# A trunk kernel with split float32 matmuls: two views of each activation tile at different SBUF offsets, and two tiles placed on other addresses

## The chip, the cores and the metric

The kernel runs on one core of a Trainium2 chip. The metric is the device time of one execution in microseconds; three runs of the kernel before were timed, and their median is the time before.

## What is computed

A decoder trunk of two layers on one sequence of 256 tokens with a model width of 2048, all in float32. Layer 0 mixes with a gated DeltaNet, layer 1 with differential attention on keys and values that are projected from the stream after layer 0. Each layer has an MLP of width 8192 with a squared ReLU, and a per-layer embedding that is projected and gated. Cut to what matters:

```python
for i in range(DEPTH):                       # DEPTH = 2
    xn = rmsnorm(h, norm_mix[i])
    if i < N_A:                              # layer 0: 16 query/key heads, 32 value heads of 128
        h = h + gated_deltanet(xn, gdn_w_in[i], gdn_conv_w[i], gdn_a_log[i], gdn_dt_bias[i], gdn_norm_w[i], gdn_w_out[i])
    else:                                    # layer 1: 8 heads, all read the shared keys and values
        h = h + diff_attention(xn, k_shared, v_shared, diff_w_q[j], ..., diff_subln_w[j], diff_w_o[j], i)
    hn = rmsnorm(h, norm_mlp[i])
    h = h + jnp.square(jax.nn.relu(hn @ mlp_w1[i])) @ mlp_w2[i]
    gate = jax.nn.sigmoid(rmsnorm(h, norm_ple[i]) @ ple_w_gate[i])
    h = h + (p[i] @ ple_w_proj[i]) * gate
    if i == N_A - 1:
        kv = rmsnorm(h, kv_norm) @ w_kv      # shared keys (2048 columns) and values (2048 columns)
return rmsnorm(h, final_norm)
```

## The kernel before

**Split products.** Every large product runs as three matmuls on values that are split in a high and a low part: high by high, high by low, low by high. `chunk` (line 116) loads 1 MB of a weight matrix into a tile `raw` by a DMA on SP's queue, and for each 1024 columns of it ScalarE writes the high part `whi` (line 130) and VectorE the low part `wlo` (line 131). `raw`, `whi` and `wlo` have three buffers each. The activations lie transposed in pairs of tiles of 128 partitions by 16 x 256 values: `xha` and `xla` (the pair `xa`, allocated in `run`), `xhb` and `xlb` (the pair `xb`, in `attention`), `hidh` and `hidl` (the hidden layer of the MLP), `oh` and `ol` (four rows of 256 values, the normalised output of two DeltaNet heads).

**Two forms of product.** In `g2` (line 136) the weights are the stationary operand, 128 columns at a time, and the activations move, 256 columns per matmul:

```python
nc.tensor.matmul(o, hi[:, k, cs], xh[:, kt], ...)   # line 149
nc.tensor.matmul(o, hi[:, k, cs], xl[:, kt], ...)   # line 150
nc.tensor.matmul(o, lo[:, k, cs], xh[:, kt], ...)   # line 151
```

In `g1` (line 154) the activations are stationary, 128 tokens at a time, and the weights move, 512 columns per matmul (lines 165 to 167). Every matmul has a weight load of its own, which loads its stationary operand.

**What runs in which form.** `g2` with `xa`: in layer 0 the gates (48 matmuls), the keys (768), the queries and values of eight groups of heads (768 and 1536); the first half of both MLPs (6144); the shared keys (768). That is 10032 matmuls. `g2` with `xb`: the query projection of layer 1 (768). `g1` with `xa`: the projection z of the eight groups (768), the gate of the embedding step `ple` in both layers (768), the shared values (384). `g1` with `xb`: the output projection of the attention, whose input `oT` is written into the pair `xb` once the queries are done (384). `g1` with `oh` and `ol`: the output projection of the DeltaNet (768). `g1` with `hidh` and `hidl`: the second half of the MLPs (6144).

**Order.** In `deltanet` a written plan sets the order of the steps: keys and inverses of triangular blocks first, then for each of eight groups the unit step `unit` (two heads in turn: a chain of small 128-column matmuls on TensorE with a subtraction on VectorE after each, lines 409 to 444), the next group's queries and values, z, and the output projection of the group before. The tile framework's scheduler orders the instructions of each engine, and it places matmuls of the next group's projections between the steps of a unit's chain. After it come MLP, `ple`, `attention`, MLP, `ple` and `final`.

**Sums of squares.** `rstd` (line 170) takes eight Square activations on ScalarE, whose elementwise output goes to a tile `junk` with two buffers, then a reduction on VectorE, a square root on ScalarE and a reciprocal on VectorE.

Of the kernel before, what the change touches and what calls it, by code (L numbers as in the profile page):

```python
# [10 lines left out]
F32 = mybir.dt.float32  # L11
# [5 lines left out]
P = 128  # L17
# [13 lines left out]
EPS = 1e-6  # L31
NEG = -1e30
LAM_INIT = 0.8 - 0.6 * math.exp(-0.3 * 1)
POST = 1.0 - LAM_INIT


class Trunk:
# [78 lines left out]
    def chunk(self, src, kn, cols):  # L116
        """src [kn*128, cols] -> list of kn*cols/1024 (hi, lo, first k tile, k tiles)"""
        nc = self.nc
        raw = self.wraw.tile([P, 2048], F32, name="raw")
        size = kn * cols  # L120
        nc.sync.dma_start(out=raw[:, :size].rearrange("p (k n) -> p k n", k=kn),
                          in_=src.rearrange("(k p) n -> p k n", p=P))
        res = []
        step = 1024 // cols
        for k0 in range(0, kn, step):
            kk = min(step, kn - k0)
            sl = raw[:, k0 * cols:(k0 + kk) * cols]
            hi = self.whl.tile([P, 1024], F32R, name="whi")[:, :kk * cols]
            lo = self.whl.tile([P, 1024], F32R, name="wlo")[:, :kk * cols]
            nc.scalar.copy(hi, sl)  # L130
            nc.vector.tensor_tensor(lo, sl, hi.bitcast(F32), ALU.subtract)  # L131
            res.append((hi.rearrange("p (k n) -> p k n", k=kk),
                        lo.rearrange("p (k n) -> p k n", k=kk), k0, kk))
        return res

    def g2(self, x, w, nk, c0, cols, kn):
        """channel-major product: returns banks, bank i holds column tiles 2i, 2i+1 as [128, 2, 256]"""
        nc = self.nc
        xh, xl = x
        nct = cols // P  # L140
        banks = [self.bank() for _ in range((nct + 1) // 2)]
        for kb in range(0, nk, kn):
            for hi, lo, k0, kk in self.chunk(w[kb * P:(kb + kn) * P, c0:c0 + cols], kn, cols):
                for k in range(kk):
                    kt = kb + k0 + k
                    for ct in range(nct):
                        o = banks[ct // 2][:, (ct % 2) * T:(ct % 2) * T + T]
                        cs = slice(ct * P, ct * P + P)
                        nc.tensor.matmul(o, hi[:, k, cs], xh[:, kt], start=kt == 0 and ct % 2 == 0, stop=False, skip_group_check=True)  # L149
                        nc.tensor.matmul(o, hi[:, k, cs], xl[:, kt], start=False, stop=False, skip_group_check=True)  # L150
                        nc.tensor.matmul(o, lo[:, k, cs], xh[:, kt], start=False, stop=kt == nk - 1, skip_group_check=True)  # L151
        return banks

    def g1(self, x, w, nk, c0, kn=4, pool=None):
        """token-major product with 512 columns from c0: returns one bank per token tile"""
        nc = self.nc
# [13 lines left out]
    def rstd(self, h, scale=1.0 / D, epscol=0):  # L170
        """reciprocal root mean square per token: [128, 2]"""
        nc = self.nc
        ss = self.small.tile([P, NT, 4], F32, name="ss")
        for b in range(4):
            for t in range(NT):
                junk = self.small.tile([P, 512], mybir.dt.bfloat16, name="junk")
                nc.scalar.activation(junk, h[t][b], AF.Square, accum_out=ss[:, t, b:b + 1])
        r = self.small.tile([P, NT], F32, name="rs", bufs=4)
        nc.vector.tensor_reduce(r, ss, axis=AX.X, op=ALU.add)
        nc.scalar.activation(r, r, AF.Sqrt, scale=scale, bias=self.eps[:, epscol:epscol + 1])  # L180
        nc.vector.reciprocal(r, r)
        return r

    def transposed(self, h, outs):
        """outs: list of (x tile, weight columns); writes hi/lo of h transposed, scaled per channel"""
        nc = self.nc
# [12 lines left out]
    def xpair(self, pool, which):  # L199
        return (pool.tile([P, KD, T], F32R, name="xh" + which), pool.tile([P, KD, T], F32R, name="xl" + which))  # L200

    def rowcast(self, r, dst):
        """[128, 2] per-token values -> dst [128, 256] along the free dimension on every partition"""
        nc = self.nc
# [7 lines left out]
    def gates(self, x, pool, tmp):  # L212
        """beta and cumulative log decay: token-major [128, 2, 64] and rows in DRAM"""
        nc, d = self.nc, self.d
# [38 lines left out]
    def conv(self, banks, dst, ch0):  # L253
        """banks of channel-major projections -> dst(i) [128, 256]: causal conv of four taps"""
        nc = self.nc
# [16 lines left out]
    def key_norms(self, half, kT, pool):  # L272
        """diagonal 32x32 blocks of the key products of eight heads; norms and row scales from their diagonals"""
        nc = self.nc
# [12 lines left out]
        nc.vector.tensor_tensor(dg, Gc, self.i32[:, None, :].to_broadcast([P, 16, 32]), ALU.mult)  # L287
        ss = pool.tile([P, 8, 2], F32, name="kss", bufs=1)
        nc.vector.tensor_reduce(ss.rearrange("p h c -> p (h c)"), dg, axis=AX.X, op=ALU.add)
# [7 lines left out]
    def invert(self, half, Gc, one, pool):  # L297
        """inverses of the 32x32 diagonal blocks of eight key heads, all value heads and both halves of the sequence"""
        nc = self.nc
# [73 lines left out]
    def unit(self, u, kT, q, qn, vt, pool):  # L373
        """one query/key head with its two value heads: normalised token-major output [128, (half, head), 128]"""
        nc = self.nc
# [217 lines left out]
    def ple(self, h, layer, w, pool):  # L593
# [11 lines left out]
        nc.vector.tensor_tensor(pl, ps, ph.bitcast(F32), ALU.subtract)  # L605
        self.transposed(h, [(self.xa, w)])
        r = self.rstd(h)
        for nb in range(4):
            gate = self.g1(self.xa, d["ple_w_gate"][layer], KD, nb * 512)
            pr = self.g1((ph, pl), d["ple_w_proj"][layer], 2, nb * 512, kn=2, pool=self.mis)  # L610
# [9 lines left out]
    def attention(self, h):  # L620
        nc, tc, d = self.nc, self.tc, self.d
        with ExitStack() as c:
            pool = c.enter_context(tc.tile_pool(name="att", bufs=2))
            one = c.enter_context(tc.tile_pool(name="att1", bufs=1))
            xb = self.xpair(one, "b")
            self.transposed(h, [(xb, self.w_mix1), (self.xa, self.w_kv)])
# [27 lines left out]
            v = [one.tile([P, D], F32, name=f"v{t}") for t in range(NT)]  # L654
            oT = xb

# [27 lines left out]
            def values(hd, aT):  # L684
# [4 lines left out]
                nc.tensor.matmul(po[:, T:], aT[:, 2 * P:], v[1][:, vs], start=False, stop=True, skip_group_check=True)  # L689
                ss = pool.tile([P, 2], F32, name="oss")  # L690
                o = pool.tile([P, 512], F32, name="o")
# [50 lines left out]
    def run(self, stop=None):  # L742
# [6 lines left out]
        self.constants()  # L749
        self.xa = self.xpair(self.main, "a")  # L750
        steps = [("mix0", lambda: self.deltanet(h))]
# [39 lines left out]
```

## Time and profile before

| | us |
|---|---|
| three runs | 2990.04, 2992.25, 2991.72 |
| median | 2991.72 |
| span of the profiled execution, first to last instruction | 2988.6 |

The profile gives the span of its execution and no separate time for it; the median of the runs is 3.1 us above the span, and that is what lies around it.

| engine | busy us | share of the span |
|---|---|---|
| TensorE, matmuls | 2951.5 | 99% |
| TensorE, weight loads | 2667.5 | 89% |
| VectorE | 1783.0 | 60% |
| ScalarE | 1449.6 | 49% |
| GpSimd | 57.9 | 2% |

How to read it: matmuls are pipelined, so one matmul's recorded time (some 280 ns for 256 columns) is longer than the distance to the next one's start, and a busy share of 99% does not tell how fast TensorE goes. Its pace, the distance from one matmul's start to the next one's, is read from a stretch that holds one kind of matmul alone: its length divided by the number of starts in it. The stages follow each other in time: the DeltaNet to about 930 us, MLP of layer 0 from 938 to 1652, `ple` to 1752, queries of layer 1 from 1774 to 1853, shared keys from 1853 to 1945, values and attention to 2083, its output projection to 2151, MLP of layer 1 from 2158 to 2872, `ple` and the end.

### The profile page before, as it was taken

Reading aid. Unit: us, or ns where it says so; the run is one execution under the profiler, and the core shown is the slowest. Engines: PE = TensorE matmul, PEld = TensorE weight load, DVE = VectorE, ACT = ScalarE, POOL = GpSimd, SP = SyncE. Lnnn points to the kernel's source line nnn. Section 1 sums busy time; section 2 is a strip of 40 time slices with the busy share of each in tenths; the row PEclk is TensorE's granted clock in tenths of the full one; section 3 lists DMA queues with packets and bytes.
Section 4 is the critical chain, followed back from the end, with each engine's and each line's share of the span. In section 5 each row is a group of like instructions: output and inputs, shape, how many; then the busy total and the mean of one; then the engine's idle time right before and its main releaser. Section 6 shows DMA issues by size and latency. Waiting matters only on the chain.

```text
span 2988.6 us, 44778 instructions
## 1 busy us (share of the span) xinstructions
PE 2951.5 (99%) x18730; PEld 2667.5 (89%) x18730; DVE 1783.0 (60%) x2324; ACT 1449.6 (49%) x1947; POOL 57.9 (2%) x64
## 2 busy tenths in 40 slices
PE   8999999999999999999999999999999999999998
PEld 8999889988988998989988889987899899898886
DVE  7879766666666555555555564467555555555555
ACT  5655555545545443444434553367444444344454
POOL 0011000000000000000000000000000000000000
PEclk9999999999999999999999999999999999999999
DMA  6654544445445555555565556544555565555654
GB/s 195 203 170 140 171 159 148 145 162 163 141 142 175 183 182 196 184 189 192 183 196 190 171 179 194 183 160 142 186 184 183 187 194 184 193 183 188 211 169 155
DMA packets 289595, 527.19 MB, mean 176 GB/s; under 512 B 25966, under 2 KB 44560, under 8 KB 289264
## 3 DMA queue, kind: packets, MB, share of 16 engines
q1 hardware_dynamic: 288160, 521.77, 54.2%
q8 instruction: 147, 2.41, 0.3%
q0 software_dynamic: 816, 2.03, 0.2%
q10 hardware_dynamic: 416, 0.53, 0.1%
q14 instruction: 56, 0.46, 0.0%
HBM read 520.03 MB, written 4.26 MB: 175 GB/s over the span
## 4 chain that ended last, share of the span: by engine, by line
PE 95%; DVE 3%; ACT 1%; DMA 1%; issue 0%; POOL 0%; ACTq 0%; SPq 0%; DVEq 0%
PE accb L165 16%; PE accb L166 16%; PE accb L167 16%; PE accb L150 14%; PE accb L151 14%; PE accb L149 14%; PE misb L426 2%; DVE wlo L131 1%; PE misb L409 1%; PE misb L431 1%; ACT whi L130 0%; PE misb L441 0%; PE misb L192 0%; PE misb L418 0%; PE misb L359 0%; ACT xha L196 0%
## 5 line engine op out<-in xcount | busy, mean ns | idle before, releaser
L131 DVE TENSOR_TENSOR wlo<-raw,whi 128x1024 fp32r<-128x1024 f32 x970 | 1189.9, 1228 | 1019.5 <-ACT whi L130 1018.4
L130 ACT CAST whi<-raw 128x1024 fp32r<-128x1024 f32 x970 | 1018.0, 1050 | 1337.3 <-PE accb L167 673.2
L149 PE MATMUL accb<-xha,whi 128*128 128x256 f32 x3344 | 953.9, 286 | 0.8 <-ACT whi L130 0.8
L150 PE MATMUL accb<-xla,whi 128*128 128x256 f32 x3344 | 952.6, 285 | 2.0 <-DVE xla L197 2.0
L151 PE MATMUL accb<-xha,wlo 128*128 128x256 f32 x3344 | 951.8, 285 | 0.2 <-DVE wlo L131 0.2
L150 PEld LDWEIGHTS accb<-xla,whi 128*128 128x128 f32 x3344 | 641.1, 192 | 2.8 <-DVE xla L197 2.6
L149 PEld LDWEIGHTS accb<-xha,whi 128*128 128x128 f32 x3344 | 640.9, 192 | 1.5 <-ACT whi L130 1.0
L151 PEld LDWEIGHTS accb<-xha,wlo 128*128 128x128 f32 x3344 | 640.7, 192 | 0.4 <-DVE wlo L131 0.4
L165 PE MATMUL accb<-whi,hidh 128*128 128x512 f32 x1024 | 398.7, 389 | 0.0
L166 PE MATMUL accb<-wlo,hidh 128*128 128x512 f32 x1024 | 398.6, 389 | 0.0
L167 PE MATMUL accb<-whi,hidl 128*128 128x512 f32 x1024 | 398.6, 389 | 0.0
L165 PE MATMUL accb<-whi,xha 128*128 128x512 f32 x640 | 253.5, 397 | 0.9 <-ACT xha L196 0.9
L166 PE MATMUL accb<-wlo,xha 128*128 128x512 f32 x640 | 252.5, 394 | 0.1
L167 PE MATMUL accb<-whi,xla 128*128 128x512 f32 x640 | 251.6, 394 | 0.0
L167 PEld LDWEIGHTS accb<-whi,hidl 128*128 128x128 f32 x1024 | 192.3, 188 | 39.9
L165 PEld LDWEIGHTS accb<-whi,hidh 128*128 128x128 f32 x1024 | 192.3, 188 | 39.8
L166 PEld LDWEIGHTS accb<-wlo,hidh 128*128 128x128 f32 x1024 | 192.3, 188 | 39.5
L165 PEld LDWEIGHTS accb<-whi,xha 128*128 128x128 f32 x640 | 120.3, 188 | 25.7 <-ACT xha L196 2.2
L166 PEld LDWEIGHTS accb<-wlo,xha 128*128 128x128 f32 x640 | 120.6, 188 | 24.9 <-DVE wlo L131 1.4
L167 PEld LDWEIGHTS accb<-whi,xla 128*128 128x128 f32 x640 | 120.2, 188 | 23.6
L165 PE MATMUL accb<-whi,oh 128*128 128x512 f32 x256 | 101.3, 396 | 0.8 <-ACT oh L466 0.8
L166 PE MATMUL accb<-wlo,oh 128*128 128x512 f32 x256 | 101.4, 396 | 0.0
(276 smaller groups left out, 2614.5 us busy)
## 6 DMA issues: line engine op xcount, KB each, us to landing
raw<-mlp_w SPq DMA_DIRECT2D x256, 1024.0 KB, 5.2
raw<-gdn_w_in SPq DMA_DIRECT2D x97, 1024.0 KB, 5.1
raw<-gdn_w_out SPq DMA_DIRECT2D x32, 1024.0 KB, 5.0
raw<-ple_w_gate SPq DMA_DIRECT2D x32, 1024.0 KB, 5.0
raw<-w_kv SPq DMA_DIRECT2D x32, 1024.0 KB, 5.3
raw<-diff_w_q SPq DMA_DIRECT2D x16, 1024.0 KB, 5.1
raw<-diff_w_o SPq DMA_DIRECT2D x16, 1024.0 KB, 5.0
gcb<-gcd SPq DMA_DIRECT2D x16, 256.0 KB, 4.3
```

The costliest lines, as they stand in the source:

```text
L130: nc.scalar.copy(hi, sl)
L131: nc.vector.tensor_tensor(lo, sl, hi.bitcast(F32), ALU.subtract)
L149: nc.tensor.matmul(o, hi[:, k, cs], xh[:, kt], start=kt == 0 and ct % 2 == 0, stop=False, skip_group_check=True)
L150: nc.tensor.matmul(o, hi[:, k, cs], xl[:, kt], start=False, stop=False, skip_group_check=True)
L151: nc.tensor.matmul(o, lo[:, k, cs], xh[:, kt], start=False, stop=kt == nk - 1, skip_group_check=True)
L165: nc.tensor.matmul(banks[t], xh[:, kt, ts], hi[:, k], start=kt == 0, stop=False)
L166: nc.tensor.matmul(banks[t], xh[:, kt, ts], lo[:, k], start=False, stop=False)
L167: nc.tensor.matmul(banks[t], xl[:, kt, ts], hi[:, k], start=False, stop=kt == nk - 1)
L409: nc.tensor.matmul(ps[:, n * P:(n + 1) * P], DB[:, n], av[:, n // 2, 2 * (n % 2)], start=True, stop=True)
L426: nc.tensor.matmul(ps[:, h * P:(h + 1) * P], NTt[:, 2 * h + c], X[:, h * P:(h + 1) * P], start=True, stop=True)
L431: nc.tensor.matmul(ps[:, h * P:(h + 1) * P], UB[:, 2 * h + c], X[:, h * P:(h + 1) * P], start=True, stop=True)
```

## The change

The pairs `xa` and `xb` get tiles that are 512 bytes longer per partition (128 values more), and `xpair` gives two views of each pair: one that starts 112 values (448 bytes) into the tile, and one that starts at its first byte. The first view takes the name `self.xa` (and `xb`) and serves everything but `ple` and the attention's output; the second view, `self.xs`, is what `ple` writes and reads, and the second view of `xb` is `oT`. So `g2` always reads the activations at the shifted start, z and the shared values read them there too, as stationary operand, and the gate of `ple` and the attention's output projection read from the unshifted start.

```diff
+SHIFT = 112
...
     def xpair(self, pool, which):
-        return (pool.tile([P, KD, T], F32R, name="xh" + which), pool.tile([P, KD, T], F32R, name="xl" + which))
+
+        tiles = [pool.tile([P, KD * T + 128], F32R, name=n + which) for n in ("xh", "xl")]
+        return tuple(tuple(t[:, o:o + KD * T].rearrange("p (k t) -> p k t", k=KD) for t in tiles) for o in (SHIFT, 0))
...
-        self.xa = self.xpair(self.main, "a")
+        self.xa, self.xs = self.xpair(self.main, "a")
...
-        self.transposed(h, [(self.xa, w)])
+        self.transposed(h, [(self.xs, w)])
...
-            gate = self.g1(self.xa, d["ple_w_gate"][layer], KD, nb * 512)
+            gate = self.g1(self.xs, d["ple_w_gate"][layer], KD, nb * 512)
...
-            xb = self.xpair(one, "b")
+            xb, oT = self.xpair(one, "b")
...
-            oT = xb
...
-                junk = self.small.tile([P, 512], mybir.dt.bfloat16, name="junk")
+                junk = self.small.tile([P, 512], mybir.dt.bfloat16, name="junk", bufs=1)
...
-        ss = pool.tile([P, 8, 2], F32, name="kss", bufs=1)
+        ss = pool.tile([P, 32], F32, name="kss", bufs=1)[:, :16].rearrange("p (h c) -> p h c", c=2)
...
-                ss = pool.tile([P, 2], F32, name="oss")
+                ss = pool.tile([P, 16], F32, name="oss")[:, :2]
```

The last three edits change sizes: `junk` gives up one of its two buffers of 1024 bytes, which pays for the longer pair `xa`, and `kss` and the attention's `oss` grow, which moves the tiles behind them. The built programs place the tiles so (byte offset in a partition, and its rest by 1024, by 512 and by 128; the weights' buffers `raw`, `whi`, `wlo` lie on multiples of 4096 in both):

```
                           before                       changed
xha as g2, z, V read it    86016    0   0   0           86464  448 448  64
xla as g2, z, V read it   102400    0   0   0          103360  960 448  64
xha as ple reads it        86016    0   0   0           86016    0   0   0
xla as ple reads it       102400    0   0   0          102912  512   0   0
xhb as g2 reads it        140736  448 448  64          141248  960 448  64
xlb as g2 reads it        157120  448 448  64          158144  448 448  64
oT, high part             140736  448 448  64          140800  512   0   0
oT, low part              157120  448 448  64          157696    0   0   0
oh                        220480  320 320  64          220544  384 384   0
ol                        224576  320 320  64          224640  384 384   0
hidh (both buffers)       122112  256 256   0          122112  256 256   0
```

In the DeltaNet most of the small tiles move by 64 bytes: `vt`, `X`, `Y`, `E`, `NTt`, `DB` and `UB` from multiples of 128 to 64 past one, `vc`, `qsq`, `o` and the keys the other way.

TensorE's instructions stand in the same order in both programs. With one buffer of `junk` the scheduler places a few instructions of VectorE and ScalarE otherwise where `ple` begins. VectorE there, before (`rs<-ss` is the reduction of `rstd`, `rs<-rs` its reciprocal, `xla<-misb,cols,xha` the low part of the transposed stream):

```order
L605 TENSOR_TENSOR pl<-misb,ph 128x512
L197 SCALAR_TENSOR_TENSOR xla<-misb,cols,xha 128x256 x13
L179 TENSOR_REDUCE rs<-ss 128x2
L131 TENSOR_TENSOR wlo<-raw,whi 128x1024
L197 SCALAR_TENSOR_TENSOR xla<-misb,cols,xha 128x256 x2
L181 RECIPROCAL rs<-rs 128x2
```

and in the changed program:

```order
L608 TENSOR_TENSOR pl<-misb,ph 128x512
L198 SCALAR_TENSOR_TENSOR xla<-misb,cols,xha 128x256 x3
L180 TENSOR_REDUCE rs<-ss 128x2
L198 SCALAR_TENSOR_TENSOR xla<-misb,cols,xha 128x256 x10
L182 RECIPROCAL rs<-rs 128x2
L132 TENSOR_TENSOR wlo<-raw,whi 128x1024
```

The reduction moves ahead of ten of the low parts, and the reciprocal ahead of one split of weights and two low parts. ScalarE at the same place, before (`junk,ss<-h` is the Square, `rs<-rs,eps` the square root):

```order
L177 ACTIVATE junk,ss<-h_81 128x512
L177 ACTIVATE junk,ss<-h_85 128x512
L196 ACTIVATE xha<-misb,cols 128x256 x10
L130 CAST whi<-raw 128x1024
L196 ACTIVATE xha<-misb,cols 128x256 x2
L180 ACTIVATE rs<-rs,eps 128x2
```

and in the changed program:

```order
L178 ACTIVATE junk,ss<-h_81 128x512
L178 ACTIVATE junk,ss<-h_85 128x512
L197 ACTIVATE xha<-misb,cols 128x256 x4
L181 ACTIVATE rs<-rs,eps 128x2
L197 ACTIVATE xha<-misb,cols 128x256 x6
L131 CAST whi<-raw 128x1024
```

The square root moves ahead of eight high parts and one cast of weights.

## Rows read from the trace of the kernel before

**Rows 1.** The page: TensorE's busy time, and its granted clock in 40 slices.

```profile
PE 2951.5 (99%) x18730; PEld 2667.5 (89%) x18730; DVE 1783.0 (60%) x2324; ACT 1449.6 (49%) x1947; POOL 57.9 (2%) x64
...
PEclk9999999999999999999999999999999999999999
```

**Rows 2.** The page: the chain that ended last, by engine, and by line.

```profile
PE 95%; DVE 3%; ACT 1%; DMA 1%; issue 0%; POOL 0%; ACTq 0%; SPq 0%; DVEq 0%
PE accb L165 16%; PE accb L166 16%; PE accb L167 16%; PE accb L150 14%; PE accb L151 14%; PE accb L149 14%; PE misb L426 2%; DVE wlo L131 1%; PE misb L409 1%; PE misb L431 1%; ACT whi L130 0%; PE misb L441 0%; PE misb L192 0%; PE misb L418 0%; PE misb L359 0%; ACT xha L196 0%
```

**Rows 3.** Groups of TensorE by line and shape: count, busy us, mean ns, idle before.

```profile
L149 PE MATMUL accb<-xha,whi 128*128 128x256 f32 x3344 | 953.9, 286 | 0.8 <-ACT whi L130 0.8
...
L165 PE MATMUL accb<-whi,xha 128*128 128x512 f32 x640 | 253.5, 397 | 0.9 <-ACT xha L196 0.9
...
L165 PE MATMUL accb<-whi,oh 128*128 128x512 f32 x256 | 101.3, 396 | 0.8 <-ACT oh L466 0.8
...
L149 PE MATMUL accb<-xhb,whi 128*128 128x256 f32 x256 | 70.7, 278 | 2.4 <-ACT xhb L196 2.4
...
L165 PE MATMUL accb<-whi,xhb 128*128 128x512 f32 x128 | 51.3, 401 | 0.0
```

**Rows 4.** Stretches of g2 alone: queries (xb), shared keys (xa), MLP of layer 0 (xa).

```profile
core 0: us, PE busy (x) PEld busy (x) DVE busy (x) ACT busy (x) POOL busy (x), PEclk, DMA share, GB/s
1780.00:1850.00 70.00, 70.00 (x620) 70.00 (x620) 35.51 (x32) 27.16 (x26) 0.00 (x0) 1.00 0.62 200
1860.00:1930.00 70.00, 70.00 (x586) 70.00 (x585) 34.36 (x31) 25.13 (x24) 0.00 (x0) 1.00 0.57 184
1210.00:1280.00 70.00, 70.00 (x585) 70.00 (x585) 36.62 (x36) 31.83 (x37) 0.00 (x0) 1.00 0.59 186
```

**Rows 5.** Timeline of TensorE in the query projection: start us, us, engine, line.

```profile
1799.89 0.28 PE L151 MATMUL accb<-xhb,wlo 128*128 128x256 f32 x1
1800.01 0.28 PE L149 MATMUL accb<-xhb,whi 128*128 128x256 f32 x1
1800.12 0.28 PE L150 MATMUL accb<-xlb,whi 128*128 128x256 f32 x1
1800.23 0.28 PE L151 MATMUL accb<-xhb,wlo 128*128 128x256 f32 x1
```

**Rows 6.** The page: the two instructions that split a chunk of weights.

```profile
L131 DVE TENSOR_TENSOR wlo<-raw,whi 128x1024 fp32r<-128x1024 f32 x970 | 1189.9, 1228 | 1019.5 <-ACT whi L130 1018.4
L130 ACT CAST whi<-raw 128x1024 fp32r<-128x1024 f32 x970 | 1018.0, 1050 | 1337.3 <-PE accb L167 673.2
```

**Rows 7.** Stretches of g1 alone: oT, MLP of layer 1 (hidh, hidl), oh twice.

```profile
2100.00:2150.00 50.00, 50.00 (x220) 41.05 (x219) 25.00 (x23) 21.41 (x26) 0.00 (x0) 1.00 0.59 190
2710.00:2760.00 50.00, 50.00 (x222) 41.44 (x221) 25.40 (x23) 19.30 (x19) 0.00 (x0) 1.00 0.59 192
426.00:446.00 20.00, 20.00 (x87) 16.14 (x86) 13.31 (x16) 8.20 (x8) 0.00 (x0) 1.00 0.64 208
527.00:545.00 18.00, 18.00 (x79) 14.52 (x78) 11.41 (x13) 7.30 (x7) 0.00 (x0) 1.00 0.64 205
```

**Rows 8.** Line 149 alone in one DeltaNet group: its unit stretch, the clean run behind.

```profile
449.40:489.20 39.80, 19.33 (x65) 12.45 (x66) 1.00 0.38 123
489.20:500.30 11.10, 8.79 (x31) 5.93 (x31) 1.00 0.47 163
```

**Rows 9.** Timeline of TensorE in that unit stretch.

```profile
456.50 0.28 PE L150 MATMUL accb<-xla,whi 128*128 128x256 f32 x1
457.05 0.71 PE L426 MATMUL misb<-X,NTt 128*128 128x128 f32 x4 [0.27 <-DVE X L428]
...
458.31 0.28 PE L151 MATMUL accb<-xha,wlo 128*128 128x256 f32 x1
458.43 0.61 PE L426 MATMUL misb<-X,NTt 128*128 128x128 f32 x4
```

**Rows 10.** Timeline of ScalarE where the first ple begins.

```profile
1657.87 2.37 ACT L196 ACTIVATE xha<-misb,cols 128x256 fp32r<-128x256 f32 x6 [0.40 <-PE misb L192]
...
1661.76 0.34 ACT L180 ACTIVATE rs<-rs,eps 128x2 f32<-128x2 f32 x1
```

## The prediction

> **What bounds the kernel now.** I read the page first: TensorE is busy for 99% of the span, and its granted clock never leaves the top tenth, 2.4 GHz [rows 1]. The chain that ended last runs through TensorE for 95% of its length, and six lines, the three of `g1` and the three of `g2`, hold some 90% of it [rows 2]. So what sets the time is the pace of the two forms of matmul. Recorded durations don't give that pace, but the groups by shape give the first hint: the same line 149, with the same shapes, takes 286 ns on `xha` and 278 ns on `xhb` [rows 3]. What differs between the two in the program is the tile and where it lies: `xha` on a multiple of 512 bytes, `xhb` 448 bytes past one.
>
> The stretches turn the hint into a pace. The projection of the queries (moving operand `xb`) and the projection of the shared keys (moving operand `xa`) stand back to back in the same layer, run the same code on weights of the same shape, and have nearly the same work on VectorE and ScalarE beside them (35.51 and 34.36 us, 27.16 and 25.13 us of 70). In 70 us the first gets 620 matmuls in, the second 586 [rows 4]. A count includes those already running at the left edge, 0.28 us by the pace or 2.4 matmuls. So the pace is 70.00 / 617.6 = 113.3 ns with `xb` and 70.00 / 583.6 = 119.9 ns with `xa`. The MLP's stretch with `xa`, in another layer and with more work on ScalarE, has 585: 120.1 ns. All three lines of the `xb` stage run alike: starts at 1799.89, 1800.01, 1800.12 and 1800.23 are 0.34 us for three, 113 ns each [rows 5].
>
> **g2 on the shifted view.** The change puts both tiles of `xa` 448 bytes past a multiple of 512, where `xb` lay before. I take the difference of the two stretches, 6.5 ns (one matmul more or less in a count moves it by 0.2), for each of the 10032 matmuls (3344 per line [rows 3], three lines): 10032 x 6.5 = 65.2 us less. Bounds from both sides: nothing, if the tile's offset is not what makes `xb` fast; 6.7 ns each, if the counts err that way (67.2 us).
>
> Is there cover that would run out? At 113.3 ns, 24 matmuls eat one chunk of 1024 weight columns in 2.72 us. The split of a chunk takes 1.05 us on ScalarE and 1.23 us on VectorE [rows 6], side by side with the chunks before and after. The query stretch already lives at that rate, with 200 GB/s of DMA [rows 4], and so does the second half of the MLP: its matmuls of 512 columns run at 227.0 ns, twelve to the chunk, 2.72 us again [rows 7]. The first half of the MLP adds some 6 us of ScalarE and 1 to 2 us of VectorE to 70 [rows 4], which leaves both near half busy. I cost the feed at nothing.
>
> **What the DeltaNet gives back.** In one group of heads line 149 has 65 matmuls between the steps of the unit's chain and 31 in the clean run behind it [rows 8]. The first lot is filler: while VectorE works on `X`, TensorE does projections. Where a step already waits (line 426 starts at 457.05, 0.55 us after the matmul before it, with 0.27 us put down to `X` of line 428), faster filler only makes the wait longer. Where the step follows its filler at once (458.31, then 458.43) the gain stays, until the slack is gone [rows 9]. Eight groups of 65 x 3 are 1560 matmuls, worth 10.1 us at 6.5 ns. Lost of that can be nothing, or all of it. I take a third, 3.4 us, because the steps of both kinds stand side by side in those rows and the waiting ones are the fewer.
>
> **g1 on the shifted view.** z and the shared values now load their stationary operand from 64 bytes past a multiple of 128. The nearest row is the attention's output projection, whose `oT` lay there before: 50.00 us hold 220 - 1.7 starts, 229.0 ns, against 222 - 1.7 or 227.0 ns with `hidh` and `hidl`, on a multiple of 256 [rows 7]. That is 2.0 ns by 1152 matmuls (768 of z, 384 of the values), 2.3 us more. The far row is `oh`, also 64 past a multiple of 128, but 320 past one of 512: 20.00 / (87 - 1.7) = 234.5 and 18.00 / (79 - 1.7) = 232.9 ns, some 6.7 ns above 227.0 [rows 7]; by it the price would be 7.7 us. Below, nothing. I take 2.3, since `oT` had the very offset (448 of 512) that the view gets.
>
> **g1 on the unshifted places.** The output projection of the attention leaves that offset: 384 x 2.0 = 0.8 us less. `oh` and `ol` come to 384 of 512, a multiple of 128 as `hidh` is: 768 matmuls (256 per line [rows 3]) by 6.7 ns, 5.1 us less, and between that and nothing if what counts is not the 128. `ple` keeps a multiple of 512: nothing.
>
> **The small edits.** The 64-byte moves of the unit's tiles touch some 1000 matmuls of 128 columns; at one nanosecond either way that is 1 us either way, and I take nothing. At the start of each `ple` the square root now stands before the high parts: 0.34 us of ScalarE, of which the 0.40 us of idleness there may hide all [rows 10]; with the reduction and reciprocal on VectorE it is between nothing and 1 us for the two layers, and I take 0.4. The Squares on one `junk` lie on ScalarE, one after another as before: nothing.
>
> **Sum.** -65.2 + 3.4 + 2.3 - 0.8 - 5.1 + 0.4 = -65.0 us. The sum is made against the profiled span of 2988.6 us, giving 2923.6; what lies around the span is 3.1 us to the median of the runs, and I leave it as it is: 2991.7 - 65.0 = 2926.7, say 2927 us.
>
> **The rivals.** *The offset is not the cause.* The rows of `xb` confound its offset with its place: `xb` begins at byte 140736, `xa` at 86016, and no row has `g2` on another tile. Then `g2` stays at 120 ns, and with the prices of `g1` alone the time is 2991.7 + 2.3 - 0.8 - 5.1 + 0.4 = 2988.5. Against it: where `g1` reads its stationary operand from `oh` at 220480 it is slow, from `hidh` at 122112 fast [rows 7], so height alone orders nothing there, and the remainder does. A rule bears on this. The Trainium skill, page "TensorE: Matmul & The Clock Gate", section "Step-by-step: what each phase is for", says that TensorE has two independent read ports on SBUF and that loading the next weights takes no read bandwidth from the running matmul. By it a start address should cost neither operand anything, the whole sum would be nothing, and the time 2991.7. The trace speaks against that reading: two stretches of equal shapes that differ by 6.6 ns a matmul [rows 4]. I give this rival 5%.
>
> *Half of the offset is not copied.* In the old `xb` both tiles stood at 448 of 1024; now `xla` stands at 960. If its matmuls (line 150, 3344) stay at 120 ns, 21.7 us of the gain go: 2948. Against it: the weights' slices alternate between 0 and 512 of 1024 in the `xb` stage, so both distances occur there, and its starts are even [rows 5]. 7%.
>
> *The shift is a cost.* In `g1` every operand that leaves a multiple of 128 makes the matmul slower, by 2.0 to 6.7 ns [rows 7]. If the same holds for the moving operand of `g2` and `xb`'s speed comes from its place, 10032 x 2.0 = 20.1 us are added: 2991.7 + 20.1 + 2.3 - 5.9 + 0.4 = 3008.6, and 3056 at 6.7 ns. It decides from about 1 ns a matmul, which would outweigh what `oh` and `oT` give. For it: three of the four rows of `g1`. Against it: the one row that shows a shifted moving operand is the fast one [rows 4]. 3%.
>
> **How the numbers follow.** The forecast, at 85%, has its own bounds: below, no loss in the DeltaNet (-3.4), 6.7 ns in place of 6.5 (-2.0) and the small tiles (-1), with some 2 us for what lies around the span: 2918. Above, all filler lost (+6.7), z and values at the price of `oh` (+5.4), no gain on `oh` (+5.1) and 1 us at `ple`: about 2945, so 2946. That range leaves out the second rival at 2948 and the other two, 15%, and a little of the forecast itself. A measurement of this kernel can tell about 0.2%, 6 us, from no change. Faster by more than that are the forecast and the half-copied offset, 0.92; within it the first rival, 0.05; slower the third, 0.03.
>
> **What would show it.** In the changed profile: `g2` on `xha` with a mean near 278 ns in place of 286; some 617 starts in 70 us of the MLP's first half and of the shared keys; `oh` near 227 ns, z and values near 229 ns; `ple` as before; more idle time of TensorE in front of lines 426 and 431. The prediction is wrong if the shared keys still run at 120 ns, if line 150 alone stays slow, or if waits on `whi` or `wlo` appear in the MLP.

## The result, and the profile after

The changed kernel takes 2950.64 us (median of four runs, 2949.39 to 2954.46) against 2991.61 us of the kernel before beside it: a ratio of 0.9867, with a 95% interval of 0.9853 to 0.988. That is 41 us less. The forecast was 65 us less, 2927 us with a range of 2918 to 2946: the sign was right, the size was not.

The page of the changed kernel, TensorE's busy time and the chain that ended last by engine and by line (lines 150 to 152 are now `g2`, 166 to 168 `g1`):

```profile
PE 2909.7 (99%) x18730; PEld 2626.2 (89%) x18730; DVE 1782.8 (60%) x2324; ACT 1451.8 (49%) x1947; POOL 60.4 (2%) x64
...
PE 93%; DVE 4%; ACT 2%; DMA 0%; issue 0%; POOL 0%; ACTq 0%; DVEq 0%
PE accb L166 16%; PE accb L167 16%; PE accb L168 16%; PE accb L151 13%; PE accb L152 13%; PE accb L150 13%; PE misb L429 2%; DVE wlo L132 1%; ACT whi L131 1%; PE misb L434 1%; PE misb L412 0%; PE misb L444 0%; PE misb L193 0%; PE misb L421 0%; DMA h<-x 0%
```

TensorE still sets the time. Where the gain lies shows stage by stage. The stretches of the changed kernel are the DeltaNet, the MLP of layer 0, the shared keys and the MLP of layer 1:

```profile
0.00:931.50 931.50, 909.42 (x6063) 823.71 (x6064) 669.01 (x1125) 502.70 (x762) 55.48 (x53) 0.99 0.51 164
931.50:1631.70 700.20, 700.20 (x4585) 640.50 (x4584) 374.64 (x358) 307.44 (x336) 0.00 (x0) 1.00 0.60 191
...
1833.50:1920.40 86.90, 86.90 (x770) 86.90 (x769) 43.94 (x41) 33.76 (x32) 0.00 (x0) 1.00 0.61 194
...
2133.10:2833.30 700.20, 700.20 (x4585) 640.48 (x4584) 374.64 (x358) 307.44 (x336) 0.54 (x1) 1.00 0.60 193
```

and the same four of the kernel before:

```profile
0.00:938.00 938.00, 919.68 (x6063) 834.05 (x6064) 668.74 (x1125) 502.71 (x762) 53.05 (x53) 0.99 0.51 163
938.00:1651.70 713.70, 713.70 (x4585) 653.93 (x4584) 374.54 (x358) 306.97 (x336) 0.00 (x0) 1.00 0.59 188
...
1853.00:1945.10 92.10, 92.10 (x770) 92.10 (x770) 44.63 (x41) 33.51 (x32) 0.00 (x0) 1.00 0.57 183
...
2158.30:2872.00 713.70, 713.70 (x4585) 653.92 (x4584) 374.57 (x358) 307.11 (x336) 0.54 (x1) 1.00 0.59 189
```

The DeltaNet is 6.5 us shorter, each MLP 13.5, the shared keys 5.2. These 38.7 us are, within 0.1, the difference of the two traced spans (2988.6 and 2950.0); the two medians lie 41 us apart, and the traced execution of the changed kernel, 2951.79 us, is one of its longer ones. By the forecast's price of 6.5 ns the shared keys should lose 768 x 6.5 = 5.0 us, which they did, and each MLP 3072 x 6.5 = 20.0 us, of which a third is missing.

The group of line 150, the first of `g2`, shows a mean in the changed kernel that lies between the two values of before (286 and 278 ns in [rows 3]):

```profile
L150 PE MATMUL accb<-xha,whi 128*128 128x256 f32 x3344 | 939.4, 281 | 0.8 <-ACT whi L131 0.8
```

A mean of 281 hides two groups. A run of `g2` here is a row of its matmuls with no other matmul between them, and its entry is where it begins. The MLP takes its hidden layer in four quarters: `g2` of the first and of the second quarter, `g1` of the first, `g2` of the third, `g1` of the second, `g2` of the fourth, and the rest of `g1`. Stretches of `g2` alone in the changed kernel, in the order of time: first and second quarter of the MLP of layer 0 (one run of `g2`), its third quarter, its fourth, the queries, the shared keys. They answer to [rows 4]:

```profile
1020.00:1090.00 70.00, 70.00 (x620) 70.00 (x619) 39.74 (x39) 33.49 (x39) 0.00 (x0) 1.00 0.62 193
1200.00:1270.00 70.00, 70.00 (x596) 70.00 (x596) 37.70 (x37) 32.38 (x37) 0.00 (x0) 1.00 0.58 182
1380.00:1450.00 70.00, 70.00 (x597) 70.00 (x596) 38.02 (x37) 32.05 (x37) 0.00 (x0) 1.00 0.61 191
1760.00:1830.00 70.00, 70.00 (x620) 70.00 (x619) 35.40 (x33) 27.42 (x26) 0.00 (x0) 1.00 0.61 199
1840.00:1910.00 70.00, 70.00 (x620) 70.00 (x619) 35.51 (x32) 26.71 (x27) 0.00 (x0) 1.00 0.61 195
```

With 2.4 matmuls off for the left edge, 620 is 113.3 ns a matmul and 596 to 597 is 117.8. The first half of the MLP runs like the old `xb`, the second half does not, with the same code, the same tile `xa` at the same place, weights of the same shape and nearly the same work beside it. The distances between neighbouring starts say the same: within a run of `g2` their mean stays at 113.3 or at 117.8 ns from the first ten matmuls to the last, for up to 1511 matmuls. The kernel before knew one pace with `xa`, 120.0 ns.

The groups of TensorE in the first of these stretches, with its weight loads (PEld), and in the second:

```profile
L151 PEld LDWEIGHTS accb<-xla,whi 128*128 128x128 f32 x207 | 38.9, 188 | 0.0
L150 PEld LDWEIGHTS accb<-xha,whi 128*128 128x128 f32 x206 | 38.7, 188 | 0.0
L152 PEld LDWEIGHTS accb<-xha,wlo 128*128 128x128 f32 x206 | 38.7, 188 | 0.0
```

```profile
L152 PEld LDWEIGHTS accb<-xha,wlo 128*128 128x128 f32 x199 | 38.2, 192 | 0.0
L151 PEld LDWEIGHTS accb<-xla,whi 128*128 128x128 f32 x199 | 37.4, 188 | 0.0
L150 PEld LDWEIGHTS accb<-xha,whi 128*128 128x128 f32 x198 | 37.2, 188 | 0.0
```

At the slower pace one weight load of three takes 192 ns in place of 188. Which of the three it is differs: in the keys of the DeltaNet (100 to 155 us), which run at 117.8 ns too, it is line 150, and with the shift at 64 bytes (below) the slower pace comes with 187 to 188 ns in all three. So the loads mark the pace here and are not shown to cause it. In the kernel before all three took 192 with `xa`, as this group shows:

```profile
L149 PEld LDWEIGHTS accb<-xha,whi 128*128 128x128 f32 x3344 | 640.9, 192 | 1.5 <-ACT whi L130 1.0 <-ACT xha L196 0.3
```

What differs between the stretches is what stood before the run. Timeline of TensorE in the changed kernel where the third quarter begins (behind `g1`), and where the unbroken run of the first quarter does (behind four small transposing matmuls):

```profile
1189.69 0.39 PE L168 MATMUL accb<-whi,hidl 128*128 128x512 f32 x1
1189.92 0.28 PE L150 MATMUL accb<-xha,whi 128*128 128x256 f32 x1
1190.04 0.28 PE L151 MATMUL accb<-xla,whi 128*128 128x256 f32 x1
```

```profile
931.14 0.63 PE L193 MATMUL misb<-ident,h 128*128 128x128 f32 x4
931.52 0.37 PE L151 MATMUL accb<-xla,whi 128*128 128x256 f32 x1
931.73 0.28 PE L152 MATMUL accb<-xha,wlo 128*128 128x256 f32 x1
```

The first goes over without a gap, and its second start already comes 0.12 us after the first. The second has 0.21 us between its first two starts, and is at 113 to 114 ns a few matmuls on.

### The profile page after: what moved, and what is told of

Its sections match the earlier page's. It is cut to its first block, busy times and chain, and to the rows that moved or that the text cites. A ratio compares the mean times of both kernels' runs of the same rounds, so it can differ in the third digit from the quotient of the medians.

```text
span 2950.0 us, 44777 instructions
## 1 busy us (share of the span) xinstructions
PE 2909.7 (99%) x18730; PEld 2626.2 (89%) x18730; DVE 1782.8 (60%) x2324; ACT 1451.8 (49%) x1947; POOL 60.4 (2%) x64
## 4 chain that ended last, share of the span: by engine, by line
PE 93%; DVE 4%; ACT 2%; DMA 0%; issue 0%; POOL 0%; ACTq 0%; DVEq 0%
PE accb L166 16%; PE accb L167 16%; PE accb L168 16%; PE accb L151 13%; PE accb L152 13%; PE accb L150 13%; PE misb L429 2%; DVE wlo L132 1%; ACT whi L131 1%; PE misb L434 1%; PE misb L412 0%; PE misb L444 0%; PE misb L193 0%; PE misb L421 0%; DMA h<-x 0%
## 5 line engine op out<-in xcount | busy, mean ns | idle before, releaser
L150 PE MATMUL accb<-xha,whi 128*128 128x256 f32 x3344 | 939.4, 281 | 0.8 <-ACT whi L131 0.8
L151 PE MATMUL accb<-xla,whi 128*128 128x256 f32 x3344 | 937.6, 280 | 1.6 <-DVE xla L198 1.6
L152 PE MATMUL accb<-xha,wlo 128*128 128x256 f32 x3344 | 936.9, 280 | 0.5 <-DVE wlo L132 0.5
L152 PEld LDWEIGHTS accb<-xha,wlo 128*128 128x128 f32 x3344 | 633.2, 189 | 0.7 <-DVE wlo L132 0.7
L151 PEld LDWEIGHTS accb<-xla,whi 128*128 128x128 f32 x3344 | 629.7, 188 | 2.4 <-DVE xla L198 2.2
L150 PEld LDWEIGHTS accb<-xha,whi 128*128 128x128 f32 x3344 | 630.4, 189 | 1.4 <-ACT whi L131 1.0
```

## Experiments

Three theories were set up on the size. **A**: a run of `g2` on the shifted view takes one of two paces at its entry, by what stands before it, and holds it. **B**: the slower pace comes from `xl`, which lies at 960 of 1024 in place of 448. **C**: the pace belongs to the quarter, to its tiles or the work beside it. Two more, **D** and **E**, on what in the offset counts, came with the second set.

### The shift alone taken back

```diff
-SHIFT = 112
+SHIFT = 0
```

> The changed kernel with SHIFT at 0, so that both views start at the first byte; every other edit stays. Both theories below agree here: g2 on xa goes back to 120.0 ns a matmul, in all its runs, and takes 41 to 42 us more than in the changed kernel, while z and the shared values come back from 229 to 227 ns, 2 us less. That gives 2989 to 2992 us, and says that the shift alone is what made the changed kernel faster. If the other edits carry a part, the time stays clearly under 2988 us.

Measured: 2993.35 us, a ratio to the kernel before of 1.0007 (0.9997 to 1.0016). Stretches of the MLP's third quarter of layer 0 and of the queries:

```profile
1210.00:1280.00 70.00, 70.00 (x585) 70.00 (x585) 37.35 (x37) 31.87 (x37) 0.00 (x0) 1.00 0.57 182
1780.00:1850.00 70.00, 70.00 (x586) 70.00 (x585) 34.30 (x31) 25.14 (x24) 0.00 (x0) 1.00 0.57 191
```

Both are at 120 ns, the queries on `xb` too, which had 620 in [rows 4]. So the offset is the cause: the shift is worth 42.7 us of the changed kernel, and the other edits nothing that can be measured. The time itself is 1.4 us above what was expected.

### The order of the MLP

```diff
-        prev = first(0)
-        for q in range(1, 4):
-            cur = first(q)
-            second(q - 1, prev)
-            prev = cur
-        second(3, prev)
+        for q in range(4):
+            second(q, first(q))
```

> The changed kernel with the MLP's loop written as first and second half of each quarter in turn, so that the second quarter's g2 now follows a run of g1 instead of the first quarter's g2. Theory A (a run of g2 on the shifted view takes one of two paces, 113.3 or 117.8 ns, in its first matmuls, by what stands before it, and holds it to its end): the second quarter, 113.3 ns in the changed kernel, now runs at 117.8 ns in both layers, 3.4 us longer each, and the first quarter stays at 113.3 ns. Theory C (the pace belongs to the quarter, by its tiles or the work beside it): the second quarter stays at 113.3 ns. In both the time rises by some 1 to 2 us at each start of a second half, which now waits for its own first half: about 2960 us by A, 2955 us by C.

Measured: 2962.68 us in one run. Stretches of the first and the second quarter in layer 0, the queries, the shared keys, the first and the second quarter in layer 1:

```profile
930.00:1000.00 70.00, 70.00 (x620) 70.00 (x620) 40.48 (x43) 33.99 (x42) 0.00 (x0) 1.00 0.61 191
1110.00:1180.00 70.00, 70.00 (x597) 70.00 (x596) 37.84 (x37) 32.23 (x37) 0.00 (x0) 1.00 0.58 181
...
1760.00:1830.00 70.00, 70.00 (x596) 70.00 (x596) 34.55 (x32) 26.32 (x25) 0.00 (x0) 1.00 0.60 196
1840.00:1910.00 70.00, 70.00 (x597) 70.00 (x596) 34.56 (x31) 26.20 (x25) 0.00 (x0) 1.00 0.58 186
2150.00:2220.00 70.00, 70.00 (x621) 70.00 (x620) 39.17 (x38) 33.19 (x38) 0.00 (x0) 1.00 0.61 194
2320.00:2390.00 70.00, 70.00 (x596) 70.00 (x596) 37.56 (x37) 32.57 (x37) 0.00 (x0) 1.00 0.59 190
```

The second quarter went from 113.3 to 117.8 ns in both layers, as A says, and C falls. The next two rows were in no theory's numbers: the queries on `xb`, the very row on which the forecast stood, run at 117.8 ns here, and the shared keys, which follow them without a gap, take that pace over.

### A break before the third and fourth quarter

```diff
+            if q >= 2:
+                ps = self.bank(512, self.mis)
+                for i in range(4):
+                    nc.tensor.transpose(ps[:, i * P:(i + 1) * P], self.ident, self.ident)
             for nb in range(4):
```

> The changed kernel with four small 128-column matmuls on the identity matrix between a run of g1 and the g2 of the third and fourth quarter of both MLPs; their result is not used. Theory A: the four runs get a new entry, and each then runs at 113.3 or at 117.8 ns from its first ten matmuls to its last, nothing between; where it is fast it saves 768 x 4.45 = 3.4 us, so between 0 and 13.7 us less, plus 1.8 us for the sixteen small matmuls: 2939 us if all four turn, 2952 us if none does. Theory C: all four stay at 117.8 ns, 2952 us.

Measured: 2939.42 us, a ratio of 0.9826 (0.9812 to 0.9841). Stretches of the third and fourth quarter in layer 0 (those in layer 1 have 620 as well):

```profile
1200.00:1270.00 70.00, 70.00 (x620) 70.00 (x620) 39.37 (x38) 32.97 (x39) 0.00 (x0) 1.00 0.61 195
1380.00:1450.00 70.00, 70.00 (x619) 69.96 (x619) 39.46 (x39) 33.53 (x40) 0.00 (x0) 1.00 0.61 195
```

All four turned to 113.3 ns, and the time is the 2939 us that A gives for that case. Sixteen matmuls whose result nobody reads, 1.8 us by the estimate, buy 13.7 by the paces; the median is 11.2 us below the changed kernel's.

### xl at 448 of 1024

```diff
-        tiles = [pool.tile([P, KD * T + 128], F32R, name=n + which) for n in ("xh", "xl")]
+        tiles = [pool.tile([P, KD * T + e], F32R, name=n + which) for n, e in (("xh", 256), ("xl", 128))]
```

> The changed kernel with 512 bytes more behind the high tile of each pair, so that xl lies at 448 of 1024 as xh does, as in the old xb. Theory B (the slow pace comes from xl at 960 of 1024): every run of g2 is at 113.3 ns, some 5000 matmuls x 4.45 ns or 22 us less: about 2929 us. Theory A: runs that follow g1 (third and fourth quarter of the MLPs) still take 117.8 ns, other runs may draw anew: 2945 to 2956 us.

Measured: 2952.38 us, a ratio of 0.987 (0.9856 to 0.9885), the changed kernel's own. The third quarter, in layer 0 and in layer 1, is where it was:

```profile
1200.00:1270.00 70.00, 70.00 (x597) 70.00 (x596) 37.46 (x38) 32.57 (x37) 0.00 (x0) 1.00 0.58 183
2400.00:2470.00 70.00, 70.00 (x597) 70.00 (x596) 37.47 (x37) 32.57 (x37) 0.00 (x0) 1.00 0.59 190
```

B falls, and with it the forecast's rival of the offset copied by half.

### Other offsets

Four kernels differ from the changed one in the number alone: `SHIFT` at 16, 64, 96 and 120, that is 64, 256, 384 and 480 bytes.

> The changed kernel with SHIFT at 16, so that the moving operand of g2 starts 64 bytes past a multiple of 512 in place of 448; every other edit stays. Theory D (what counts is the rest by 128, 64 bytes as with 448): g2 has the same two paces, 113.3 and 117.8 ns, with 117.8 after g1; z and the shared values at 229 ns; 2945 to 2956 us. Theory E (the distance from the weights' slice by 512 counts, and 448 is 64 before the next slice while 64 is 64 behind it): another pace, at best one that all runs share, at worst 120.0 ns everywhere, 2990 us.

Measured: 2964.93 us in one run. Second and third quarter of layer 0:

```profile
1020.00:1090.00 70.00, 70.00 (x620) 70.00 (x619) 40.55 (x41) 35.56 (x42) 0.00 (x0) 1.00 0.62 196
1200.00:1270.00 70.00, 70.00 (x597) 70.00 (x596) 37.83 (x37) 32.58 (x37) 0.00 (x0) 1.00 0.59 186
```

The same two paces as at 448, but the time lies above D's range: in this run more entries ended at the slower one, among them all the longer ones of the DeltaNet and the queries. z took 233.3 ns in place of the expected 229.

> The changed kernel with SHIFT at 64, 256 bytes, a multiple of 128 but half of 512. Theory D: a multiple of 128, so g2 is back at 120.0 ns in all runs and z and the shared values at 227 ns: 2988 to 2993 us. Theory E: at the largest distance from the weights' slice, g2 is at 113.3 ns or faster in all runs: 2925 to 2935 us.

Measured: 2994.51 us in one run, 227 ns for z and the shared values, and 120 ns in the second quarter of layer 0:

```profile
1020.00:1090.00 70.00, 70.00 (x586) 70.00 (x585) 36.90 (x36) 32.31 (x37) 0.00 (x0) 1.00 0.57 182
```

> The changed kernel with SHIFT at 96, 384 bytes, the offset that oh and ol have in the changed kernel. Theory D: 120.0 ns in all runs of g2, 2988 to 2993 us; z and the shared values at 227 ns, and then the 232 ns of oh at the same offset must come from something else than its address. Theory E: a pace of its own below 120.0 ns, and z and the shared values near the 232 ns of oh.

Measured: 2989.69 us in one run. Second and third quarter:

```profile
1020.00:1090.00 70.00, 70.00 (x593) 70.00 (x591) 37.38 (x37) 32.20 (x37) 0.00 (x0) 1.00 0.57 181
1220.00:1290.00 70.00, 70.00 (x585) 70.00 (x585) 37.40 (x37) 31.95 (x37) 0.00 (x0) 1.00 0.57 183
```

70.00 / (593 - 2.4) is 118.5 ns, behind `g1` it is 120: again two paces by the entry, other ones. z and the shared values took 232 to 233 ns, near `oh` at the same offset. So D, the rest by 128, does not hold: 384 is a multiple of 128 and behaves unlike 0 and 256 for both operands. E does not hold as it was put either, since 256 gives nothing.

> The changed kernel with SHIFT at 120, 480 bytes, 32 before a multiple of 512. If only the 64-byte half of 128 counts, as 64, 448 (two paces) against 0 and 256 (120.0 ns) suggest, 480 lies in the upper half as 448 does and g2 has the same two paces, 113.3 and 117.8 ns: 2945 to 2965 us. If each 32 bytes count, g2 gets a pace of its own between 110 and 120 ns. z and the shared values: 229 ns or above.

Measured: 2982.16 us in one run. Second and third quarter have one pace, 70.00 / (594 - 2.4) = 118.3 ns, so 480 is not 448: it has a pace of its own between 110 and 120, as the second reading had it. z and the shared values took 233 ns. The second (the third has 594 as well):

```profile
1020.00:1090.00 70.00, 70.00 (x594) 70.00 (x593) 37.97 (x37) 32.35 (x37) 0.00 (x0) 1.00 0.59 186
```

### oh and ol on multiples of 512

```diff
-        self.tokg = pool.tile([P, NT, 64], F32, name="tokg")
+        self.tokg = pool.tile([P, NT * 64 + 32], F32, name="tokg")[:, :NT * 64].rearrange("p (c h) -> p c h", c=NT)
```

> The changed kernel with 128 bytes more in the tile ahead of oh, so that oh and ol lie on multiples of 512 in place of 384 past one. If the address is what holds the output projection of the DeltaNet at 232.4 ns, it goes to 227 ns as the stationary operands on multiples of 512 and 256 do: 768 x 5.4 = 4.1 us less, 2946 us, give or take what new entries of g2 in the DeltaNet change. If it is its stage (four rows of 128 per bank, and other work beside it), it stays at 232 ns and the time at 2951 us.

Measured: 2947.11 us, a ratio of 0.9856 (0.984 to 0.9872). The output projection of the DeltaNet in this kernel:

```profile
421.00:441.00 20.00, 20.00 (x90) 16.52 (x89) 13.63 (x16) 8.72 (x10) 0.00 (x0) 1.00 0.62 193
```

That is 20.00 / 88.3 = 226.5 ns, the pace of `g1` on every multiple of 256 here. The address held it, not its stage. The median is 3.5 us below the changed kernel's, near the 4.1 us expected, though the two intervals overlap; the pace is the proof, the time alone would not be.

### Both together, a shorter break, and a break without a shift

The first of these takes the four small matmuls and the moved `oh` together:

> The changed kernel with the four small matmuls ahead of the third and fourth quarter and with oh and ol on multiples of 512. If the two gains add, 2950.6 less 11.2 (measured with the small matmuls) less 3.5 to 4.3 (measured with oh): 2935 to 2936 us, the four quarters at 113.3 ns and oh at 226.7 ns. If entries in the DeltaNet fall otherwise, up to 4 us to either side. If the small matmuls turned the four runs by luck, one or more of them is back at 117.8 ns, 3.4 us each.

Measured: 2936.94 us (2934.91 to 2943.57), a ratio of 0.9824 (0.9809 to 0.9839). The four quarters are at 113.3 ns, `oh` at 226.7 (mean of its start-to-start distances). It is the lowest median of all kernels here, 13.7 us under the changed kernel and 53 us under the kernel before beside it (2990.04), but its interval overlaps that of the break alone.

The second has one small matmul in place of four:

> The same with one small matmul in place of four. If any break in the row of g1 and g2 gives a new entry that ends fast, the four quarters are at 113.3 ns and the time is 1.3 us below that with four. If what counts is how the break ends (its length, its number), they may all stay at 117.8 ns: 13.7 us above, 2948 us.

Measured: 2940.41 us, a ratio of 0.9834 (0.9818 to 0.985). Third quarter of layer 0, queries, shared keys:

```profile
1200.00:1270.00 70.00, 70.00 (x620) 70.00 (x619) 39.37 (x38) 33.55 (x40) 0.00 (x0) 1.00 0.61 196
...
1750.00:1820.00 70.00, 70.00 (x597) 70.00 (x596) 34.58 (x31) 25.70 (x26) 0.00 (x0) 1.00 0.57 191
1830.00:1900.00 70.00, 70.00 (x597) 70.00 (x596) 33.91 (x32) 26.33 (x25) 0.00 (x0) 1.00 0.59 193
```

One small matmul is enough for the MLP. The 1.3 us it saves don't show: the median is 3.5 us above that with four, and the two intervals overlap. In the traced execution, 2938.1 us and the fastest of its four, the queries, where nothing was edited, took the slower pace, and the shared keys went on with it: 1536 x 4.5 = 6.9 us. Its DeltaNet, on the other hand, ended 3.2 us sooner than in the trace with four. So one trace does not explain the median.

The third is the kernel before with the four small matmuls:

> The kernel before, unshifted, with the same four small matmuls ahead of the third and fourth quarter. If the breaks only choose between the paces that the offset allows, g2 on xa stays at 120.0 ns in all quarters and the time is 1.8 us above the kernel before: 2993 us. If a break makes g2 faster by itself, whatever the offset, the four quarters go below 120 ns: down to 2972 us.

Measured: 2992.41 us in one run. Third quarter of layer 0 (the fourth has 586 too):

```profile
1215.00:1285.00 70.00, 70.00 (x586) 70.00 (x585) 37.14 (x37) 31.53 (x36) 0.00 (x0) 1.00 0.59 186
```

120 ns as without them. In these runs the offset says which paces there are, and the entry decides between them.

## Why the prediction was wrong

**What bounds the kernel: right.** TensorE's pace set the time before and after, and the chain shows it.

**g2 on the shifted view: the step that failed.** The prediction took "the difference of the two stretches, 6.5 ns, for each of the 10032 matmuls". The offset was the cause, as it said, and the pace of 113.3 ns is real. But 620 matmuls in 70 us of the old `xb` [rows 4] were one run of `g2` with one entry. As evidence for a pace they were one draw, however many matmuls they held; the bounds around 6.5 ns (nothing, or 6.7) came from the resolution of a count and from doubting the cause, and no bound asked whether another run on that offset would go the same way. The runs showed a second pace, 117.8 ns, 2.2 ns below 120.0 in place of 6.7. In all, the term of 65.2 us measured 41.8 in the traces: 27.0 in the two MLPs, 5.2 in the shared keys, 9.6 in the DeltaNet. Both MLPs have half of their `g2` behind `g1`, and all 22 such entries in the kernels with 64 or 448 bytes and no break took it (four each in the changed kernel and those with `xl` at 448, with 64 bytes and with the moved `oh`, six in the one with the other order). At 113.3 ns those halves would have brought 2 x 1536 x 4.5 = 13.8 us more. In the DeltaNet the distances from start to start of `g2`, summed, went from 381.0 to 371.4 us, 9.6 us less where this term had 3120 x 6.5 = 20.3. There too the runs have two paces. Of its 77 shorter runs (8 to 29 matmuls) 43 were at 118 ns behind their first few matmuls and 34 at 113 to 116, by the starts in the trace, where the kernel before had 118 to 120. In the changed kernel its keys ran at 117.8 ns (511 matmuls in 60 us of one stretch), while the clean run of the group at 485 us had 113.3 ns (73 in 8 us):

```profile
95.00:155.00 60.00, 60.00 (x511) 60.00 (x511) 49.93 (x88) 32.97 (x39) 0.00 (x0) 1.00 0.64 196
487.00:495.00 8.00, 8.00 (x73) 8.00 (x72) 3.90 (x6) 4.88 (x7) 0.00 (x0) 1.00 0.43 133
```

That the shared keys met the forecast is luck of the queries' entry, whose pace they take: in three other kernels (the other order, 64 bytes, one small matmul) both ran at 117.8 ns. Of the signs of being wrong that the prediction named, none appeared; all of them look for 120 ns or for waits, and none for a second pace.

By the spans, 26.4 us of the forecast's 65.0 are missing: 13.0 in the MLPs and 14.0 in the DeltaNet, where `oh` (below) has 4.4 of them, and the other stages differ by less than 1 us together.

**The feed: right.** The stretch at 113.3 ns in the MLP had VectorE at 39.74 and ScalarE at 33.49 us of 70, and TensorE waited for no weights there.

**What the DeltaNet gives back: near in size, but not by the mechanism.** Waits of the unit's chain on `X` went from 1.6 to 2.3 us by the list of waits, not 3.4 us more. The small matmuls of the DeltaNet took 2.8 us longer by their distances, but 2.1 of them are three waits in its first 60 us, on the constants, the normalised stream and the gates, which vary by about as much between the kernels here.

**g1 on the shifted view: right in this kernel.** z and the shared values were to go from 227.0 to 229.0 ns. Stretches of `oh`, of the attention's output projection and, last, of the shared values in the changed kernel, as in [rows 7]:

```profile
422.00:442.00 20.00, 20.00 (x88) 16.23 (x87) 13.37 (x15) 8.32 (x9) 0.00 (x0) 1.00 0.65 202
2065.00:2115.00 50.00, 50.00 (x223) 41.40 (x221) 25.51 (x23) 22.67 (x31) 0.00 (x0) 1.00 0.59 189
...
1921.00:1941.00 20.00, 20.00 (x89) 16.43 (x88) 8.97 (x8) 8.02 (x8) 0.00 (x0) 1.00 0.65 206
```

The last row is 20.00 / 87.3 = 229.1 ns, and z has 228.8 to 229.2 by its distances. This price too was read from one run: in four runs of other kernels the same offset gave 233.3 ns (last table). The attention's output projection came from 229.0 to 226 ns, near the forecast's 227.

**oh: wrong.** The step took 6.7 ns off for reaching a multiple of 128. The first of the three rows is 20.00 / 86.3 = 231.7 ns against 234.5 and 232.9 before; by the mean of distances it went from 233.3 to 232.4, 0.7 us in all in place of 5.1. The rows of before that looked right, 0 and 256, were multiples of 256 as well, and the run with multiples of 512 brought the whole gain.

**The small edits: right.** The kernel without the shift is the kernel before, within its interval.

**The rivals.** The first (the offset is not the cause) fell with the shift taken back, the second (`xl`) with its own run, the third has no row left. None of them was that the same offset has two paces, and the range, which had room for bounds within one pace, ended 4.6 us below the result. The rule weighed there stands in the Trainium skill, page "TensorE: Matmul & The Clock Gate", section "Step-by-step: what each phase is for": weight loads take no read bandwidth from a running matmul. What the prediction drew from it, that a start address costs nothing, is not what the rows show: with the shift at 0 or 256 bytes `g2` is at 120.0 ns in every run, and at 64 or 448, one number in the source, it is at 113.3 or 117.8. Whether the loads take read bandwidth, or the address acts in another way, no run here shows.

**Still open.** Why the offset sets the paces, and what at an entry picks one. Behind `g1` it was always the slower one, behind one or four small matmuls in the MLP always the quicker (12 of 12), in the DeltaNet and at the queries either, and there the same entry fell differently from kernel to kernel. Four runs of each kernel at 448 bytes lie 4.3 to 8.7 us apart, where thirteen of the kernel before lie 5.0 apart and ten with the shift at 0 lie 3.5. That would fit entries that fall differently from execution to execution, but only one execution of each kernel has a trace, so it is argued and not shown.

## What to carry to other kernels

A pace that is read from one run of equal instructions is one observation, however many instructions it holds: look for a second run with another entry before multiplying it by a count. Where a kernel is bound by back-to-back matmuls, try the start of the moving operand against the weights' (here 64 or 448 bytes past a multiple of 512), keep stationary operands on multiples of 256 (both tried, 0 and 256 past a multiple of 512, were the fast ones), and break a seam between two forms of matmul with one small one, then read the pace of every run for itself. A rule for addresses that is read off two good cases (0 and 256) has to be tried on the case that it is used for (384).

## What was not expected of the hardware

In these kernels TensorE's pace at equal shapes depends on where the operands start, and partly on what ran before. The mean distance from start to start, in ns, over runs of at least 40 matmuls without gaps, by the offset past a multiple of 512 (weights on multiples of 512 throughout):

| offset, bytes | activations moving (256 columns) | activations stationary (weights move, 512 columns) |
|---|---|---|
| 0 | 120.0 | 226.7 to 227.7 |
| 64 | 113.3 or 117.8 | 233.3 |
| 256 | 120.0 | 226.7 to 227.6 |
| 320 | not tried | 233.3 |
| 384 | 118.7 or 120.0 | 232.2 to 233.4 |
| 448 | 113.3 or 117.8 | 229, and 233.3 in four runs |
| 480 | 118.3 | 233.1 to 233.4 |

Where two values stand for the moving activations, a run keeps the one at which it settled within its first ten matmuls, and the shared keys, a run of `g2` that follows the queries' without a gap, had the queries' pace in every kernel where both start at the same offset.
